# A written-out order of a decoder layer, rewritten with the buffers' spots in it: 45 steps moved by a few places

## The chip, the cores and the metric

The kernel runs on one core of one Trainium2 chip. The core has engines that work side by side, each through its own instructions in order: TensorE (PE in the profile, its weight loads PEld) multiplies matrices, VectorE (DVE) and ScalarE (ACT) do elementwise work, GpSimd (POOL) does some more of it, and SyncE (SP) issues most of the DMA transfers. An instruction waits until what it reads is there and what it overwrites is no longer needed. The metric is the time of one execution on the device in microseconds, as the median of several runs.

## The reference, cut to what matters

The kernel computes one layer of a decoder for 512 positions of width 1024, in float32:

```python
h = rms_norm(x, attn_pre_norm)
mix = hybrid_mixer(h, ...)           # w_in; differential attention (4 heads) and
                                     # sparse attention (8 heads, 3 branches); w_out
x = x + rms_norm(mix, attn_post_norm)
h = rms_norm(x, ffn_pre_norm)
f = (silu(h @ w_gate) * (h @ w_up)) @ w_down      # inner width D_FF = 2816
x = x + rms_norm(f, ffn_post_norm)

def rms_norm(x, g):
    return x * rsqrt(mean(x * x, axis=-1) + 1e-6) * g
```

## The kernel before, in words

All products on TensorE take a value as a high part and a low part, so that float32 accuracy is kept: ScalarE copies the value into a rounded tile (`high_...`, `..._hi`), VectorE subtracts that copy from the value (`low_...`), and TensorE adds up high x high, low x high and high x low.

The first half of the execution, up to about 270 us, is the norm, the projection `w_in` in column groups, the two kinds of attention and the output projection. The second half is the norms and residual between the two, in four row tiles of 128 positions, and the channel mixer. The channel mixer works on 22 tiles of 128 of the inner width (f = 0 to 21):

- `load_ff` loads the gate and up weights of tile f (each 128x1024, 512 KB, line 421), `sum_ff` forms sums and differences of their halves on VectorE (lines 1548 to 1555), `high_ff` (ScalarE, 1568) and `low_ff` (VectorE, 1576) cut them. The products of a gate and an up tile are made from seven `block` products instead of eight (1591). The blocks are numbered 1 to 7, each made of three groups of four matmuls; block 4 is the one with the operand `d` (`dh`, `dl` in the profile), whose third group needs `low_ff.f.d`.
- `snap_1` and `snap_2` copy accumulators out of PSUM (ScalarE, 1621 for the second), `sum_x` (1610) and `sums` (VectorE, 1626) add such a copy to an accumulator, `gate_x` and `gate_c` apply silu, `mult` (1632) multiplies. `sums.f` reads the bank `yz` of tile f, into which block.f.4 afterwards adds its own product: block.f.4 has to wait for `sums.f`.
- For the down projection two tiles of f are taken as a pair p (0 to 8), again by sums and seven products. `pair_sums` adds the activations of the pair (1652) and sends one tile and one sum to DRAM (1654, 1658), to be read back later by `load_b` and `load_s4` (1756). `load_d.f` (421) and `load_22.p` (1676, half a tile) load the down weights; `sums_a.p.0` to `.2` (1682, 1684, 1688) form sums of them. `left_a` and `right_a` cut activations and weights (on VectorE lines 1699 and 1708), `high_d` and `low_d` (1720) the weight tiles as they are, `cut_act` (1792) and `cut_b` further parts. `product_a` and `product_b` are the products (1665). The four tiles f = 18 to 21 also have direct products (`down`, 1814).
- `last_sum`, `last_square`, `last_mean`, `last_gain`, `last_root`, `last_row` are the last norm and residual, by row tile i and column half c.

The norm between (rows i = 0 to 3) has the steps `sa`, `va`, `ra` (`square`, `mean`, `root` of the mixed rows, VectorE line 1454 adding two partial sums of squares of ScalarE), `gu` (`scale_post`, 1477), `re` (residual, with a store), `sb`, `vb`, `rb`, `pr` (`scale_pre`, 1484), `tr` (eight transposes on TensorE, 1514), and `h...`, `l...` (`put_high`, `put_low`, 1507), which cut the transposed rows.

Loaded weight tiles lie in three buffers of the name `wraw`, so a load waits until the last reader of its buffer's former content is done; the high and low parts `whi`, `wlo` have three each as well. Other tiles have a place in tables (`HOMES`, `S_HOMES`), one letter for each use in turn.

No scheduler orders the work. Two long strings of step names, `PLAN` (1387 steps, the attention half) and `PLAN_NORM` with `PLAN_END` (1198 steps, from the norm on) are run from left to right, and each step issues its instructions when it is called. Thus the string gives each engine, and each queue of DMAs, its order. An SP transfer that waits for its buffer holds all transfers behind it in SP's queue; the same is true of VectorE and ScalarE.

Of the kernel before, what the change touches and what calls it, by code (L numbers as in the profile page):

```python
# [61 lines left out]
v0d2 fR10 F11.0 F11.1 pW0 Kh11 D0LD1 KX11 F11.2 F12.0 KX00 Kl11 Kp11 D0S10 D0S11 fR11 D0S12 D0Q12 v0d1 pA5 pH5 D0Q11
pL5 D0X12 KW12 Kh12 Kl12 D0X13 D0Q10 F12.1 F12.2 fL13 fh13 F13.0 fl13 F13.1 F13.2 KW13 Kh13 fR12 D0LD0 Kl13 KX12
Kp12 fL14 D0S00 KX13 Kp13 fR13 fh14 D0S01 KW00 fl14 pA6 D0E13 F14.0 F14.1 Kh00 F14.2 Kl00 fL6 fh6 D0X10 KX01 D0X11
pW5 pH6 D0E12 KW01 Kh01 F6.0 fl6 pL6 D0E11 v0a0 Kl01 D0E10 D0R Kp00 Kp01 KX03 K21 fR14 fL15 fh15 fl15 KW02 Kh02 Kl02
F6.1 pW6 KX02 KO1 F15.0 N0LD F6.2 fR6 KW03 Kh03 Kl03 fL7 F15.1 F15.2 fR15 pA7 N0K1 fh7 Kp02 Kp03 N0S11 D0S02 KO0 KT0
# [20 lines left out]
LW5 v1d3 N3PH N3E10 N3E11 D2Q00 D2X02 D2S10 D2X00 D2X01 N2T00 D2Q11 D2Q10 D2X11 D2X12 D2E02 D2X10 N2H00 N2T02 N2H02
N2L02 N2T01 N2H01 N2L00 D2S12 N4LD N2L01 N1V10 N1V11 N1V12 D2E12 D2Q12 D2X13 N2M10 N2T10 D2E11 N1O1 D2E10 N3M01
N3S12 N2H10 N1O2 N4SC N1OH W6a N4CX N4CA N3PL N3Q12 N2TC N3X13 N2HC N2L10 N2T11 N2H11 D2E13 N3M03 v1p2.0 D2E00 N2L11
N1OL N3S11 D2R N5LD N5SC W1h N3Q11 N5CX D2E01 N3TC D2g N3X12 N2T12 D2MX2 D2MX0 N4K0 D2MX1 N3E13 N3E12 N3R1 N3g1  # L90
v1p2.1 v1a2 v1d2 N3M11 N2H12 N3HC N4S01 N4CE N4K1 N4S1 N3T02 W5h W5l N4Q01 N2L12 N4Q1 N4X11 N4X01 N4E01 N2V00 N4X02
# [2055 lines left out]
```

## Time and profile before

| | |
|---|---|
| median of 3 runs | 623.32 us (621.71 to 624.0) |
| the profiled execution | 622.45 us, span 620.5 us |
| mean granted TensorE clock | 0.994 |
| PE busy | 607.1 us (98%) |
| DVE busy | 546.4 us (88%) |
| ACT busy | 373.9 us (60%) |
| POOL busy | 101.4 us (16%) |
| moved by DMA | 98.41 MB, mean 159 GB/s |

How to read it: the span runs from the first to the last instruction of the profiled execution, and its 1.95 us more are outside of that. "Busy" is the sum of an engine's instructions. A row of the timeline shows the start, the length, the engine, the line of the kernel, the operation, out<-in by the program's names, the shape, how many instructions are taken together (x8), and in brackets the idle time just before and what ended it. SPq is the queue of SP, where a row is the issue of a transfer.

### The profile page before, as it was taken

To read this page: it belongs to the slowest core of one execution; us is meant where nothing else is said; L and a number is where in the kernel's file an instruction comes from. 1 tells how busy PE (TensorE), PEld (TensorE's weight loads), DVE (VectorE), ACT (ScalarE), POOL (GpSimd) and SP (SyncE) were. 2 spreads that over 40 slices of the span, in tenths; PEclk is the share of its full clock that TensorE was granted. 3 is DMA by queue.
4 is the path that set the end of the run, shared out by engine and by line. 5 is a ranking of instruction groups with operands and counts; after the bars stand their busy time and mean duration, and the time that the engine had idled before them with its cause. 6 is when DMAs were issued, how large, how long until landed. Compare 5 with 4: busy or idle time off the path is not lost. (4 is left out here: it accounts for less than half of the span.)

```text
span 620.5 us, 10992 instructions
## 1 busy us (share of the span) xinstructions
PE 607.1 (98%) x4065; PEld 549.9 (89%) x4065; DVE 546.4 (88%) x965; ACT 373.9 (60%) x784; POOL 101.4 (16%) x153
## 2 busy tenths in 40 slices
PE   9999999999999999999999999999999799999995
PEld 5888888899999988889999999999999788878884
DVE  5898898997898884999999998899999699899977
ACT  6445375467999986577584565446464365577522
POOL 0030000307868878100000000000000000000000
PEclk9999999999999999999999999999999989999998
DMA  8566986646233211545143434353531554677413
GB/s 263 187 224 248 299 296 230 216 146 248 101 119 101 88 34 63 182 165 203 59 146 104 156 117 136 119 178 121 175 102 54 174 165 140 201 222 252 135 41 130
DMA packets 38341, 98.41 MB, mean 159 GB/s; under 512 B 4240, under 2 KB 11792, under 8 KB 37392
## 3 DMA queue, kind: packets, MB, share of 16 engines
q1 hardware_dynamic: 38144, 97.59, 47.3%
q8 instruction: 32, 0.52, 0.3%
q14 instruction: 21, 0.17, 0.1%
q10 hardware_dynamic: 144, 0.13, 0.1%
HBM read 82.10 MB, written 15.60 MB: 157 GB/s over the span
## 5 line engine op out<-in xcount | busy, mean ns | idle before, releaser
L1867 POOL TENSOR_TENSOR uf<-c,gain 128x512 f32<-128x512 f32 x1 | 1.3, 1277 | 360.1 <-DVE c L1836 360.1
L1055 ACT ACTIVATE p<-sc,nm 128x512 f32<-128x512 f32 (+3 forms) x96 | 50.2, 530 | 14.4 <-DVE nm L1051 12.9
L1051 DVE TENSOR_REDUCE nm<-sc 128x1 f32<-128x384 f32 (+3 forms) x96 | 43.4, 483 | 8.6 <-PE sc L1047 5.5
L1591 PE MATMUL yz<-rope,wbh 128*128 128x256 f32 x352 | 48.0, 280 | 0.0
L1224 POOL TENSOR_TENSOR p<-p,l 128x256 f32<-128x256 f32 (+3 forms) x64 | 45.3, 732 | 1.0
L1591 PEld LDWEIGHTS yz<-rope,wbh 128*128 128x128 f32 x352 | 44.1, 191 | 0.1
L1085 DVE TENSOR_TENSOR ptl<-tr,pth 128x384 fp32r<-128x384 f32 (+1 forms) x60 | 34.3, 592 | 8.4 <-ACT pth L1082 8.4
L1082 ACT ACTIVATE pth<-tr 128x384 fp32r<-128x384 f32 (+1 forms) x60 | 29.9, 530 | 7.3 <-PE tr L1072 6.8
L1568 ACT ACTIVATE whi<-wraw 128x1024 fp32r<-128x1024 f32 x22 | 23.2, 1057 | 13.3 <-DMA wraw<-in_wg 12.5
L1568 ACT ACTIVATE wbh<-wraw 128x1024 fp32r<-128x1024 f32 x22 | 23.3, 1057 | 12.6 <-DVE wraw L1555 7.7
L1576 DVE TENSOR_TENSOR wel<-e,weh 128x1024 fp32r<-128x1024 f32 x22 | 26.7, 1219 | 3.9 <-ACT weh L1568 2.6
L1568 ACT ACTIVATE weh<-e 128x1024 fp32r<-128x1024 f32 x22 | 23.2, 1056 | 8.0 <-DVE e L1550 6.9
L1072 PE MATMUL tr<-ident,p 128*128 128x128 f32 x200 | 27.8, 274 | 0.0
L1714 ACT ACTIVATE whi<-wraw 128x1024 fp32r<-128x1024 f32 x20 | 21.0, 1057 | 10.9 <-PE acc L1665 5.7
L1591 PE MATMUL yz<-rope,wbl 128*128 128x256 f32 x176 | 27.2, 276 | 0.0
L1576 DVE TENSOR_TENSOR wlo<-wraw,whi 128x1024 fp32r<-128x1024 f32 x22 | 26.8, 1217 | 0.0
L1576 DVE TENSOR_TENSOR wbl<-wraw,wbh 128x1024 fp32r<-128x1024 f32 x22 | 26.7, 1217 | 0.0
L1720 DVE TENSOR_TENSOR wlo<-wraw,whi 128x1024 fp32r<-128x1024 f32 x20 | 24.1, 1218 | 1.1 <-ACT whi L1714 1.1
L1621 ACT ACTIVATE us<-yz 128x512 f32<-128x512 f32 x22 | 13.0, 592 | 18.7 <-PE yz L1591 15.7
L1591 PEld LDWEIGHTS yz<-rope,wbl 128*128 128x128 f32 x176 | 23.4, 188 | 0.0
L1041 PE MATMUL sc<-kst,qst 128*128 128x384 f32 (+3 forms) x64 | 23.0, 367 | 0.3 <-DMA kst<-qk 0.3
L1072 PEld LDWEIGHTS tr<-ident,p 128*128 128x128 f32 x200 | 22.4, 141 | 0.7
(382 smaller groups left out, 1993.9 us busy)
## 6 DMA issues: line engine op xcount, KB each, us to landing
wraw<-in_wg SPq DMA_DIRECT2D x24, 512.0 KB, 3.7
wraw<-in_wu SPq DMA_DIRECT2D x22, 512.0 KB, 3.4
wraw<-in_wd SPq DMA_DIRECT2D x22, 512.0 KB, 3.7
qk<-rope SPq DMA_DIRECT2D x7, 1024.0 KB, 5.9
kst<-qk SPq DMA_DIRECT2D x24, 256.0 KB, 4.2
wraw<-in_wf SPq DMA_DIRECT2D x10, 512.0 KB, 4.2
wraw<-in_wo SPq DMA_DIRECT2D x8, 512.0 KB, 4.4
qst<-qk SPq DMA_DIRECT2D x16, 256.0 KB, 2.7
```

The lines of the kernel that those rows point to most:

```text
L1041: pe.matmul(sv[i], lhs, kk[:, 0, :w], start=(n == 0), stop=False, skip_group_check=True)
L1051: dve.tensor_reduce(nm[i], sv[i], AX.X, OP.max, negate=True)
L1055: act.activation(pp[i], sv[i], AF.Exp, bias=nm[i], accum_out=hs["l"][:, row, i:i + 1])
L1072: pe.transpose(tr[:, n * P:(n + 1) * P], pp[i][:, j * P:(j + 1) * P], ident)
L1082: act.activation(part(u, 0), tv[u], AF.Copy)
L1085: dve.tensor_tensor(part(u, 1), tv[u], f32(part(u, 0)), OP.subtract)
L1224: pool.tensor_tensor(p, p, hs["l"][:, 1 + br, i:i + 1].to_broadcast(list(p.shape)), OP.mult)
L1568: act.activation(t[0], w[src], AF.Copy)
L1576: dve.tensor_tensor(t[1], W[f][PARTS[n][0]], f32(t[0]), OP.subtract)
L1591: pe.matmul(o, W[f][w][wi][:, k * P:(k + 1) * P], hop[h][hi][:, k * HS:(k + 1) * HS], start=(n < 3 and m == 0), stop=(m == 11), skip_group ...
L1714: act.activation(hi, oa[f]["raw"], AF.Copy)
L1720: dve.tensor_tensor(lo, o["raw"], f32(o["w"][0]), OP.subtract)
```

## The change: what it does

The tables of places go. Each step of the two plans names the buffers that it takes itself, as letters behind a colon (`low_d.2:1` takes the spot 1 of its kind), and a new class hands them out. The addresses are the same as before. With the plans rewritten in this way, the order in each engine's own list stays the same for TensorE and GpSimd, and changes a little for three others:

- **SP, 5 of 215 transfers:** `load_s4.1` goes behind `load_22.1` and `load_d.2`. LW1 (a weight of the output projection) goes behind pW3's transfer, `load_ff.3.g` goes two places ahead, in front of the store of re2 and xL3, the store of re3 behind load_ff.2.u, and the row of `last_row.1.1` behind that of last_row.1.0.0.
- **VectorE, 36 of 858 steps.** In the order of the work: Kl13, fR7 and N7CM of the attention's projections and copies by one or two places, N5CX two places down (behind N3X12 and D2MX2); sum_ff.1.1 one down; `gu2` behind l0.11 and sa2, sa2 itself behind l0.11; ra2 and rb2 one down; `sum_x.3` five down, behind sum_ff.4.4; sum_ff.4.3, sums.1 (three), sum_ff.6.4, sum_x.6, sum_ff.8.4, sum_x.5, sum_x.12 (two), pair_sums.3.1 down; sum_ff.18.2 two up; sums.16, mult.13, pair_sums.6.1, low_ff.19.e down; mult.16 four up; `low_d.2` one down, behind `sums.18`; sums_a.4.2 and right_a.7.1.1 one down; `sums_a.8.2` one and `right_a.7.0.1` two down, both behind `right_a.8.1.1`, the latter also behind low_d.16; cut_act.18.1, cut_b.2.2.1 and low_d.13 one down; last_gain.3.0 behind last_mean.3.0, last_sum.0.1 behind last_gain.0.0, `last_gain.1.0` behind last_mean.1.1, last_row.1.1 behind last_row.1.0.0.
- **ScalarE, 4 of 624 steps:** fh10 and Kh13 one down (behind the rotations KX10, KX12), D3LE two up, gate_x.14 one down, behind high_ff.18.e.

The core of the diff (in the plan's lines some neighbours are written in another order that changes no engine's list):

```diff
-wL2 tr00 sb1 h0.11 vb1 rb1 pr11 pr10 h0.12 mx26 mx27 gu2 tr11 kl00 sa2 tr10 mx34 l0.11 h1.11 mx35 mx32 mx33 mx36
...
-pair_sums.6.3 load_s4.1 left_a.0.0.0 load_22.1 left_a.0.0.1 right_a.0.0.0 left_a.2.0.0 pair_sums.7.2 snap_2.21
...
-block.20.6 high_ff.21.b low_ff.21.b block.19.2 high_ff.19.d low_ff.19.d load_d.2 sums_a.1.0 pair_sums.6.4
...
-right_a.1.1.0 right_a.1.1.1 sums_a.1.2 high_d.2 low_ff.21.d low_d.2 high_ff.18.d sums.18 low_ff.18.d block.19.4
...
-right_a.8.1.0 cut_b.2.1.0 low_d.3 sums_a.8.1 sums_a.8.2 high_d.16 right_a.7.0.1 load_b.0 right_a.8.1.1 product_a.7.7
...
-last_square.1.0.1 last_gain.1.0 last_mean.1.1 last_root.1 last_row.1.1 last_row.1.0.0 last_row.1.0.1
...
+kl00:i mx27 tr11:72 l0.11 sa2:4 gu2:8 tr10 mx34 mx35 h1.11 va2 load_ff.3.g:1 mx32 wH0:21 l0.12 mx33 ra2 wH2:10 re2 xL3:d
...
+high_d.0:1 block.21.6 left_a.0.0.0:h9 sums.17:z right_a.0.1.1 block.17.4 load_22.1:1 low_d.0:0 right_a.0.0.0
+left_a.2.0.0 snap_2.21:n pair_sums.7.1:d load_d.2:0 pair_sums.6.3 block.20.6 left_a.0.0.1 high_ff.21.b:gi
+high_ff.19.d:ut gate_c.17 pair_sums.7.2 gate_x.17 load_s4.1:w low_ff.21.b low_ff.19.d block.19.2:5 block.20.5
+block.21.2:3 sums_a.1.0 pair_sums.6.4:x pair_sums.7.4 snap_2.20:4 high_ff.20.d:st mult.17 load_d.4:2 sums_a.1.1
...
+high_ff.18.d:yv sums.18:0 low_d.2:1 low_ff.18.d sums_a.2.0 block.21.3 right_a.2.1.0:1i block.20.3 block.18.4 block.20.7
...
+low_d.3:2 sums_a.8.1 cut_b.2.1.0:4 high_d.16:1 product_a.7.7 load_b.0:t load_kept.3:f right_a.8.1.1 sums_a.8.2:5
+product_a.8.7 low_d.16:0 left_a.8.0.0 right_a.7.0.1 product_a.8.1 cut_b.1.0.0:c left_a.8.0.1 right_a.8.0.0 product_a.8.5
...
+last_square.1.0.0 last_mean.1.0 last_sum.1.0.1 last_square.1.0.1 last_mean.1.1 last_gain.1.0 last_root.1 last_row.1.0.0
+last_row.1.1 last_row.1.0.1
...
+class Spots:
+
+
+    def __init__(self, pool, tags, turn):
+        self.pool, self.tags, self.turn = pool, tags, turn
...
+    def tile(self, shape, dt, tag=None, name=None, bufs=1):
+        if tag in self.tags:
+            return self.pool.tile(shape, dt, tag=f"{tag}.{next(self.turn[0])}", name=name, bufs=1)
+        return self.pool.tile(shape, dt, name=name, bufs=bufs, **({"tag": tag} if tag else {}))
...
+    def run(plan):
+        for step in plan:
+            name, _, spots = step.partition(":")
+            turn[0] = iter(spots)
+            ops[name]()
+            assert not list(turn[0]), step
...
-    for tok in plan:
-        ops[tok]()
+    run(plan)
```

More of the change, by code (lines that the diff above doesn't have):

```diff
@@ L62 @@
[L62 to L66, printed above, removed]
@@ L87 @@
[L87 to L91, printed above, removed]
@@ L177 @@
-block.19.3 high_ff.21.e low_ff.21.e gate_c.14 sum_x.15 gate_x.15 mult.14 sum_x.17 block.21.1 high_ff.21.d
-sum_ff.21.3 gate_c.15 mult.15 block.21.5 snap_1.21 load_22.0 snap_1.20 load_d.0 sums_a.0.0 right_a.0.1.0 sums_a.0.1
-sums_a.0.2 block.19.7 sums.19 block.20.2 block.21.6 sums.17 block.17.4 right_a.0.1.1 high_d.0 low_d.0 pair_sums.7.1
-pair_sums.6.3 load_s4.1 left_a.0.0.0 load_22.1 left_a.0.0.1 right_a.0.0.0 left_a.2.0.0 pair_sums.7.2 snap_2.21
-block.20.6 high_ff.21.b low_ff.21.b block.19.2 high_ff.19.d low_ff.19.d load_d.2 sums_a.1.0 pair_sums.6.4
@@ L182 @@
-pair_sums.7.4 gate_c.17 gate_x.17 mult.17 block.20.5 snap_2.20 high_ff.20.d block.21.2 sums_a.1.1 sum_x.20 load_d.4
-right_a.1.1.0 right_a.1.1.1 sums_a.1.2 high_d.2 low_ff.21.d low_d.2 high_ff.18.d sums.18 low_ff.18.d block.19.4
-block.21.7 load_22.2 load_d.6 sums_a.2.0 right_a.2.1.0 gate_c.19 block.21.3 sums.21 sums_a.2.1 block.20.3 sums_a.2.2
-left_a.6.0.0 right_a.2.1.1 block.18.4 gate_c.18 block.20.7 product_a.0.5 block.21.4 low_ff.20.d sums.20 block.20.4
-left_a.0.1.0 high_d.4 low_d.4 load_22.3 gate_c.21 cut_b.3.2.0 left_a.5.0.0 left_a.0.1.1 product_a.0.7 left_a.2.1.1
@@ L197 @@
-left_a.5.1.1 product_a.5.1 sums_a.6.0 sums_a.6.1 sums_a.6.2 product_a.4.7 product_a.5.7 right_a.6.1.0 load_d.14
-right_a.6.1.1 left_a.6.0.1 cut_b.5.1.0 high_d.12 low_d.12 load_s4.0 cut_b.0.2.0 cut_b.0.2.1 load_22.7 right_a.5.0.1
-sums_a.7.0 left_a.7.0.0 cut_b.4.2.0 sums_a.7.1 load_b.2 right_a.6.0.0 right_a.6.0.1 load_d.16 sums_a.7.2
-product_a.5.6 right_a.7.1.0 right_a.7.1.1 product_a.6.5 left_a.6.1.0 left_a.6.1.1 cut_b.2.2.0 high_d.14 low_d.14
-left_a.7.1.1 gate_x.18 product_a.6.1 mult.18 gate_x.19 load_b.7 left_a.7.0.1 cut_act.18.0 left_a.8.1.1 product_a.6.7
@@ new lines @@
+block.21.2:3 sums_a.1.0 pair_sums.6.4:x pair_sums.7.4 snap_2.20:4 high_ff.20.d:st mult.17 load_d.4:2 sums_a.1.1
+right_a.1.1.0:db sum_x.20:x right_a.1.1.1 block.19.4 sums_a.1.2 block.21.7 load_22.2:1 high_d.2:2 low_ff.21.d
+high_ff.18.d:yv sums.18:0 low_d.2:1 low_ff.18.d sums_a.2.0 block.21.3 right_a.2.1.0:1i block.20.3 block.18.4 block.20.7
+gate_c.19:5 left_a.6.0.0:85 product_a.0.5:27 gate_c.18 sums.21:2 block.21.4 sums_a.2.1 load_d.6:0 sums_a.2.2:g
+left_a.0.1.0 right_a.2.1.1 low_ff.20.d sums.20:v high_d.4:0 block.20.4 low_d.4:2 left_a.0.1.1 left_a.2.1.1 load_22.3:1
```

564 lines of the change are left out of this document (223 added, 341 removed).

## The prediction

> **What bounds the kernel now.** I read the busy shares first, then TensorE's list of waits, then the timelines of TensorE, VectorE and the SP queue around the one large wait.
>
> ```profile
> span 620.5 us, 10992 instructions
> ## 1 busy us (share of the span) xinstructions
> PE 607.1 (98%) x4065; PEld 549.9 (89%) x4065; DVE 546.4 (88%) x965; ACT 373.9 (60%) x784; POOL 101.4 (16%) x153
> ```
>
> TensorE is busy for 607.1 of 620.5 us, and the change leaves its order as it is. So a moved step can only shorten a wait of TensorE, or make one. Its waits by releaser (total, times, longest):
>
> ```profile
> PE yz L1591 <- DVE vs L1626: 3.4, 1, 3.4
> PE warm L543 <- DVE warm L540: 1.2, 1, 1.2
> PE yz L1591 <- DVE wlo L1576: 0.5, 1, 0.5
> ```
>
> Only one is worth much. TensorE's timeline there (start, length, shape, what it waited for):
>
> ```profile
> 491.02 1.07 PE L1591 MATMUL yz<-rope,wbh 128*128 128x256 f32 x8
> 491.92 0.62 PE L1591 MATMUL yz<-rope,wbl 128*128 128x256 f32 x4
> 495.96 0.74 PE L1591 MATMUL yz<-x22h,dh 128*128 128x256 f32 x4 [3.42 <-DVE vs L1626]
> 496.50 1.06 PE L1591 MATMUL yz<-x22l,dh 128*128 128x256 f32 x4
> 497.36 1.05 PE L1591 MATMUL yz<-x22h,dl 128*128 128x256 f32 x4
> 498.21 1.86 PE L1591 MATMUL yz<-rope,wbh 128*128 128x256 f32 x8
> 499.91 0.64 PE L1591 MATMUL yz<-rope,wbl 128*128 128x256 f32 x4
> ```
>
> block.18.4 could have started at 491.92 + 0.62 = 492.54 and starts at 495.96, because `sums.18` (line 1626) must first have read the bank. And then TensorE is slow for 3.4 us. The windows (length, busy time and count of PE, PEld, DVE, ACT, POOL, then the granted clock):
>
> ```profile
> 489.10:492.50 3.40, 3.40 (x31) 3.24 (x29) 2.37 (x6) 2.41 (x4) 0.00 (x0) 1.00 0.59 182
> 492.60:495.90 3.30, 0.00 (x0) 0.00 (x0) 3.30 (x6) 0.34 (x1) 0.00 (x0) 1.00 0.32 119
> 496.50:499.90 3.40, 3.40 (x18) 3.40 (x17) 3.37 (x6) 2.73 (x6) 0.00 (x0) 0.50 0.35 129
> ```
>
> The clock is 0.50 there. Eight of these products took 491.92 − 491.02 = 0.90 us before the wait. The sixteen from 496.50 to 499.91 took 3.41 instead of 2 × 0.90 = 1.80: 1.61 lost, and about 0.1 more in the group at 495.96 (0.54 to the next start instead of 0.45). The place costs 3.42 + 1.7 = 5.1 us in all.
>
> [...]
>
> Why VectorE is late: the SP queue's timeline; then what two loads of a down tile took from issue to landing (last column), the first issued at 482.58, the second a lone one issued between 469.5 and 473; then VectorE.
>
> ```profile
> 481.69 0.33 SPq L1756 DMA_DIRECT2D s4b<-s  x1
> 482.11 0.38 SPq L1676 DMA_DIRECT2D wraw<-in_wd  x1
> 482.58 0.38 SPq L421 DMA_DIRECT2D wraw<-in_wd  x1
> ```
>
> ```profile
> wraw<-in_wd SPq DMA_DIRECT2D x1, 512.0 KB, 5.6
> ```
>
> ```profile
> wraw<-in_wd SPq DMA_DIRECT2D x1, 512.0 KB, 3.4
> ```
>
> ```profile
> 479.96 1.22 DVE L1720 TENSOR_TENSOR wlo<-wraw,whi 128x1024 fp32r<-128x1024 f32 x1
> ```
>
> ```profile
> 488.25 0.69 DVE L1682 TENSOR_TENSOR wraw<-wraw 128x512 f32<-128x512 f32 x1 [3.73 <-DMA wraw<-in_wd]
> ```
>
> ```profile
> 493.99 1.22 DVE L1720 TENSOR_TENSOR wlo<-wraw,whi 128x1024 fp32r<-128x1024 f32 x1
> 495.13 0.68 DVE L1626 TENSOR_TENSOR vs<-yz,us 128x512 f32<-128x512 f32 x1
> 495.73 0.68 DVE L1576 TENSOR_TENSOR dl<-d,dh 128x512 fp32r<-128x512 f32 x1
> ```
>
> `load_s4.1` (line 1756) stands first in the queue and waits for block.17.4's memory until 481.69; `load_22.1` (1676) and `load_d.2` (421) are behind it. load_d.2 goes out at 482.58, though its buffer was free when `low_d.0` ended: 479.96 + 1.22 = 481.18. It lands at 482.58 + 5.6 = 488.2, VectorE idles 3.73 us before sums_a.1.0 (488.25), and all that follows on VectorE is late. Right ahead of sums.18 stands `low_d.2` (493.99), which nothing needs so soon.
>
> **The change, part by part.**
>
> *The queue.* `load_s4.1` moves behind load_22.1 and load_d.2. load_d.2 then goes out at 481.21, 1.37 earlier, and load_22.1 before it. How long it flies no row shows. The bounds are 5.6 (as now, between two others) and 3.4 (the lone one); I take 4.0, near the lone one, because the 256 KB store and load that crowd it now start after it and only load_22.1, ahead of it, shares its way. It lands at 485.21, 0.04 after it sums_a.1.0 starts: 488.25 − 485.25 = 3.0 earlier; I count S = 2.95 (bounds 1.35 and 3.55). What cover is left: VectorE has other work until 484.5, so a landing earlier than that would gain nothing.
>
> *low_d.2 behind sums.18.* sums.18 moves up by 495.13 − 493.99 = 1.14. With both, it ends at 495.13 + 0.68 − 2.95 − 1.14 = 491.72, before 492.54: no wait. block.18.4's third group needs `low_ff.18.d`, which ends now at 495.73 + 0.68 = 496.41 and then at 493.46; at full speed the third group starts 492.54 + 2 × 0.45 = 493.44. Just in time. So 5.1 us are free at this place; with a flight of 5.6, low_ff.18.d ends at 495.06 and a wait of some 1.6 is left, too short, going by what is seen here after 3.42, to be sure of a slow clock.
>
> *What is late next.* TensorE, 5.1 earlier from here, meets the next VectorE limit. From 496 to 550 VectorE stays close behind. Where it waits for TensorE now, it gains back more than S:
>
> ```profile
> 500.58 0.69 DVE L1626 TENSOR_TENSOR vs<-yz,us 128x512 f32<-128x512 f32 x1 [0.38 <-PE yz L1591]
> ```
>
> ```profile
> 514.36 0.69 DVE L1699 TENSOR_TENSOR sl<-s,sh 128x512 fp32r<-128x512 f32 x1 [0.39 <-PE acc L1665]
> ```
>
> Both waits shrink, since TensorE gains more than VectorE: 2.95 + 0.38 + 0.39 = 3.72 by 515. The point where TensorE then stops is product_a.8.7, whose third operand comes from `right_a.8.1.1`:
>
> ```profile
> 544.94 0.69 DVE L1688 TENSOR_TENSOR t<-wraw 128x512 f32<-128x512 f32 x1
> 545.55 0.68 DVE L1708 TENSOR_TENSOR tl<-t,th 128x512 fp32r<-128x512 f32 x1
> 546.15 0.68 DVE L1708 TENSOR_TENSOR tl<-wraw,th 128x512 fp32r<-128x512 f32 x1
> ```
>
> ```profile
> 546.13 0.39 PE L1665 MATMUL acc<-th,sh 128*128 128x512 f32 x1
> 546.36 0.40 PE L1665 MATMUL acc<-th,sl 128*128 128x512 f32 x1
> 546.89 0.50 PE L1665 MATMUL acc<-tl,sh 128*128 128x512 f32 x1
> ```
>
> At a start every 0.23 us TensorE would take it at 546.59 and gets it 0.30 late, at 546.89. In the change `sums_a.8.2` (544.94) and `right_a.7.0.1` (545.55) go behind right_a.8.1.1: 546.15 − 544.94 = 1.21 earlier on VectorE, of which 0.30 goes to that lateness. TensorE can so come 1.21 − 0.30 = 0.9 more than VectorE's gain: 3.72 + 0.9 = 4.6. That is under 5.1, so the place at 546 caps it. I take 4.6; with S at its bounds 1.35 and 3.55 it is 1.35 + 0.77 + 0.9 = 3.0 and, past the cap, 5.1.
>
> *gu2 behind sa2.* VectorE:
>
> ```profile
> 276.54 0.16 DVE L1454 TENSOR_TENSOR cols<-cols 128x1 f32<-128x1 f32 x1 [0.82 <-ACT pre L1452]
> ```
>
> ```profile
> 292.94 0.74 DVE L1484 SCALAR_TENSOR_TENSOR pre<-x,cols,gain 128x512 f32<-128x512 f32 x1
> ```
>
> ```profile
> 293.21 1.18 PE L1514 MATMUL trh<-ident,pre 128*128 128x128 f32 x8
> ```
>
> ```profile
> 315.64 0.62 PE L1591 MATMUL yz<-x11l,whi 128*128 128x256 f32 x4
> 316.36 0.74 PE L1591 MATMUL yz<-x11h,wlo 128*128 128x256 f32 x4
> ```
>
> The two products of `gu2` (scale_post, 1477) now fill time before sa2's wait for ScalarE (0.82); behind it they leave that much more idle time, less the 0.69 subtraction that steps into it. I put VectorE 0.7 late from there (bounds 0 and 0.82). scale_pre ends at 293.68, 0.05 before the second four transposes, so TensorE may stop 0.65 at 293. Two later waits of TensorE take that up: the 0.5 of the list above (low_ff.16.a, its line 1576), which is shorter when TensorE comes later, and at 316, where the third group starts 316.36 − 315.64 − 0.45 = 0.27 late for low_ff.4.a; there `sum_x.3`, moved five places down, lets low_ff.4.a come sooner. Together 0.77. I cost it at 0, and at 0.65 if that cover is gone.
>
> *The rest.* N5CX goes behind D2MX2, which waits for GpSimd's D2g; no wait of TensorE's list is for line 1208: 0 to 0.2. The other VectorE, ScalarE and SP steps (Kl13, fR7, N7CM, the sum_ff, sum_x and sums neighbours, mult.13 and .16, left_a and cut_b, fh10, Kh13, D3LE, gate_x.14, LW1, re3's store, load_ff.3.g) swap with one to four neighbours, each late or early by that neighbour's length (0.2 to 1.22); no wait of TensorE over 0.5 stands by any of them. In the tail, last_mean.1.1 goes ahead of last_gain.1.0, which frees the root and the last rows by a tenth, and last_row.1.1 goes behind last_row.1.0.0: −0.1 to +0.2, taken as 0.
>
> **The sum** is −4.6 + 0 + 0 = −4.6. The profiled execution of before is 622.45 (span 620.5 and 1.95 around it); it becomes 617.85. It stands 0.87 under the median of 623.32, so the median becomes 623.32 − 4.6 = **618.7**. Its own range, with the bounds of the flight: 623.32 − 5.1 = 618.2 to 623.32 − 3.0 = 620.3.
>
> **The rivals.**
>
> *A: the wait goes, the slow clock isn't part of the gain.* The timed runs may not have it, or it may fall elsewhere. For it: the runs before differ by 2.3 us (621.71 to 624.0), more than the 1.7 that it costs. Against it: the wait of 3.42 must be in each of them, by the same order. Only the wait is then gained: 623.32 − 3.4 = 619.9.
>
> *B: load_d.2 lands no sooner.* If the DMA engines, and not the queue, set the landing at 488.2 (5.6 us for a load that takes 3.4 alone says that they are shared), sums_a.1.0 stays at 488.25. Only low_d.2's move is left, and the third group still waits for low_ff.18.d at 496.41: the wait is split, not removed. TensorE gains the first two groups done meanwhile, 2 × 0.45 = 0.9 at most: 622.4, or, with half of that lost to the slow clock, 622.9. Against it: the DMA share in the windows is 0.32 to 0.59, not near full.
>
> *C, the other side: gu2's lateness reaches TensorE and stays.* VectorE, 0.7 late behind gu2, stops TensorE for 0.65 at 293. If the two waits don't take it up (VectorE may be as late there, and then they only move along) and the place at 492 returns nothing, the time is 623.32 + 0.65 = 624.0. It decides from the point where VectorE is over 0.05 late at 293.68 and what 492 returns is under 0.65. For it: 0.05 is little room. Against it: load_d.2 is free to go 1.37 sooner, twice that sum.
>
> *That the change doesn't do what it says* (another address, and so another wait) would show as a new wait anywhere; I give it a part of C's chance.
>
> **How the numbers follow.** Forecast 0.66, A 0.12, B 0.14, C with the last 0.08. The predicted time is the forecast's, 618.7. The range leaves out most of B and C (under 0.2): 617.0 (the 5.1 in full, and 1.2 for how the three runs before lie about their median) to 622.0 (the forecast's and A's upper ends and 1.7 of that spread and of flights between 4.0 and 5.6). About 0.5%, 3.1 us, is what a measurement here can tell from no change: 620.2 and below is faster. The forecast lies there in 0.93 of its cases, A in 0.6: 0.66 × 0.93 + 0.12 × 0.6 = 0.69. Slower by 3.1 takes C and a new stop with a slow clock after it: 0.05. The remaining 0.26 is the same.
>
> **What would show it.** In the changed profile, load_d.2's row should be issued at about 481.2 and ahead of s4b's; VectorE's idle time before line 1682 at 485.3 should be 0.8, not 3.73; the list of TensorE's waits should have no vs row of 3.4, and no window near 496 a clock of 0.50. TensorE should run 5.1 ahead until 540 and keep 4.6 after 546, with a wait of about half a us for `tl`, line 1708. A landing at 488, a large wait of L1591 for `dl`, or TensorE late at 293 and still late at 450, would each prove a step wrong.

## The result, and the profile after

The changed kernel took 617.03 us (median of 4 runs, 616.62 to 618.48), the kernel before 623.28 beside it: a ratio of 0.9907, 95% interval 0.9883 to 0.9932. Timed again later beside other kernels it took 616.95 against 623.48: 0.9897 (0.9873 to 0.9920). It is faster by 6.3 to 6.5 us where 4.6 were forecast; 617.03 lies 0.03 inside the low end of the range, the second median just outside it. Of the timed runs below one, of g4, was slow throughout (667.49 us at a mean clock of 0.948); it stands in that kernel's median but not in its ratio, and its trace is not used.

The profiled execution took 618.48, the slowest of the four. The page's head and TensorE's waits:

```profile
span 616.6 us, 11000 instructions
## 1 busy us (share of the span) xinstructions
PE 605.2 (98%) x4065; PEld 548.2 (89%) x4065; DVE 545.2 (88%) x965; ACT 373.8 (61%) x784; POOL 101.0 (16%) x153
```

```profile
PE yz L1475 <- DVE vs L1510: 1.3, 1, 1.3
PE warm L425 <- DVE warm L422: 1.2, 1, 1.2
PE fm L590 <- ACT whi L577: 0.9, 1, 0.9
PE yz L1475 <- DVE dl L1460: 0.5, 1, 0.5
```

The lines of the second half have moved up by 116: 1475 is the former 1591, 1510 the former 1626, 1460 the former 1576 (and 310 is the helper at 421). The wait of 3.4 us for `vs` has become one of 1.3 and one of 0.5 for `dl`, and the 0.5 for `wlo` is down to 0.2. The 0.9 at line 590 (F13.0, at 72 us) belongs to this execution: the same kernel profiled again (f1) doesn't have it. TensorE's timeline at the place:

```profile
491.59 0.62 PE L1475 MATMUL yz<-rope,wbl 128*128 128x256 f32 x4
493.47 0.71 PE L1475 MATMUL yz<-x22h,dh 128*128 128x256 f32 x4 [1.27 <-DVE vs L1510]
494.02 0.63 PE L1475 MATMUL yz<-x22l,dh 128*128 128x256 f32 x4
495.11 0.72 PE L1475 MATMUL yz<-x22h,dl 128*128 128x256 f32 x4 [0.46 <-DVE dl L1460]
495.67 1.07 PE L1475 MATMUL yz<-rope,wbh 128*128 128x256 f32 x8
```

and the windows (length, PE, PEld, DVE, ACT, POOL, clock, DMA share, GB/s):

```profile
491.15:494.56 3.41, 2.14 (x18) 1.86 (x16) 3.38 (x6) 0.31 (x1) 0.00 (x0) 1.00 0.37 123
494.56:497.97 3.41, 2.95 (x22) 2.68 (x22) 3.38 (x6) 2.19 (x6) 0.00 (x0) 1.00 0.47 154
497.97:501.38 3.41, 3.41 (x28) 3.33 (x27) 3.41 (x6) 2.32 (x6) 0.00 (x0) 1.00 0.55 186
```

The clock stays at 1.00; the eight products at 495.67 take 0.91 to the next start, against the 0.90 at full speed in before. What led there, the SP queue, the flight of load_d.2 and VectorE:

```profile
480.04 0.33 SPq L1560 DMA_DIRECT2D wraw<-in_wd  x1
481.18 0.33 SPq L310 DMA_DIRECT2D wraw<-in_wd  x1
481.56 0.42 SPq L1640 DMA_DIRECT2D s4b<-s  x1
```

```profile
wraw<-in_wd SPq DMA_DIRECT2D x1, 512.0 KB, 5.1
```

```profile
486.38 0.69 DVE L1566 TENSOR_TENSOR wraw<-wraw 128x512 f32<-128x512 f32 x1 [1.89 <-DMA wraw<-in_wd]
...
490.37 0.42 DVE L1494 TENSOR_TENSOR act<-x,snap 128x256 f32<-128x256 f32 x1 [1.42 <-DMA s<-s]
...
492.63 0.69 DVE L1510 TENSOR_TENSOR vs<-yz,us 128x512 f32<-128x512 f32 x1
493.24 1.21 DVE L1604 TENSOR_TENSOR wlo<-wraw,whi 128x1024 fp32r<-128x1024 f32 x1
494.37 0.68 DVE L1460 TENSOR_TENSOR dl<-d,dh 128x512 fp32r<-128x512 f32 x1
```

load_22.1 and load_d.2 go out at 480.04 and 481.18, s4b behind them, as forecast. But the flight is 5.1 us, VectorE still idles 1.89 and begins 1.87 sooner, not 2.95. Then `sum_x.20` (490.37) idles 1.42 for the store of s4. In f1, the same kernel again, load_d.2 flew 4.2:

```profile
wraw<-in_wd SPq DMA_DIRECT2D x1, 512.0 KB, 4.2
```

Where TensorE gains, place by place, can be read by the start of the same step in each trace. The table gives that start less its start in the profile of before, in us (minus: earlier). e1, e2 and e4 are the experiments below, f1 is the changed kernel profiled a second time, f3, f4 and g1 are variants of it.

| step | before, at | e1 | e2 | changed | f1 | e4 | f3 | f4 | g1 |
|---|---|---|---|---|---|---|---|---|---|
| F10.0 | 52.52 | −0.28 | −0.43 | −0.37 | −0.69 | −0.38 | −0.54 | −0.54 | −0.44 |
| D0T2 | 122.98 | −0.28 | +0.59 | +1.09 | −0.73 | +0.06 | +0.05 | −0.58 | −0.08 |
| D0MS | 147.08 | −0.31 | +0.59 | +0.68 | −1.13 | −0.37 | −0.35 | −1.01 | −0.52 |
| tr20 | 286.87 | −0.25 | +0.53 | +0.71 | −1.18 | −0.20 | −0.47 | −1.14 | −0.36 |
| tr30 | 293.73 | −0.25 | +0.55 | +0.62 | −1.27 | −0.29 | +0.40 | −1.23 | −0.45 |
| block.15.5 | 416.26 | +0.37 | +0.64 | +0.67 | −1.04 | −0.13 | +1.01 | −1.34 | −0.07 |
| block.16.2 | 425.22 | +0.67 | +0.38 | +0.17 | −1.84 | −0.93 | +0.21 | −2.14 | −0.16 |
| block.20.6 | 481.50 | +0.77 | +0.66 | −0.34 | −2.35 | −1.44 | −0.30 | −2.65 | −0.67 |
| product_a.0.5 | 500.38 | −3.13 | −0.63 | −3.35 | −6.20 | −1.06 | −4.17 | −7.94 | −4.02 |
| product_a.6.1 | 537.78 | −3.14 | −0.66 | −3.06 | −5.92 | −0.71 | −3.93 | −6.82 | −3.80 |
| down_piece.21.1 | 612.66 | −3.39 | −1.06 | −3.47 | −6.33 | −1.13 | −4.34 | −7.23 | −4.22 |

Up to 123 us the columns differ by up to 1.8 us with no pattern by kernel; that is how one execution differs from the next (the changed kernel itself is at +1.09 and, in f1, at −0.73), and it is why the profile of the changed kernel (+1.09 there) shows less than the times. Differences between two rows of one column are what counts. From 481 to 500 the changed kernel gains 3.0 and 3.85. But it also gains some 0.4 between 123 and 147, 0.5 to 0.8 at 425 and about 0.5 from there to 481. The first is in no profile of the old order, and none of these gains more than 0.3 at 425; of the last e3, which has the old order there, shows 0.4 too (+1.55 to +1.16), so it may not be the change's.

### The profile page after: what moved, and what is told of

The parts are those of the page before. It is cut to its first block, busy times and chain, and to the rows that moved or that the text cites. A ratio compares the mean times of both kernels' runs of the same rounds, so it can differ in the third digit from the quotient of the medians.

```text
span 616.6 us, 11000 instructions
## 1 busy us (share of the span) xinstructions
PE 605.2 (98%) x4065; PEld 548.2 (89%) x4065; DVE 545.2 (88%) x965; ACT 373.8 (61%) x784; POOL 101.0 (16%) x153
## 4 chain that ended last, share of the span: by engine, by line
PE 31%; DVE 15%; DMA 3%; issue 2%; ACT 1%; DVEq 0%; ACTq 0%
PE yz L1475 15%; PE acc L1549 12%; PE x L1475 2%; DMA wraw<-in_wd 2%; DVE wbl L1460 1%; DVE wlo L1460 1%; PE acc L1698 1%; DVE wel L1460 1%; DVE c L1720 1%; DVE wlo L1604 1%; DVE uf L1755 1%; DVE e L1432 1%; DMA wraw<-in_wg 1%; DVE dl L1460 1%; DVE e L1434 1%
```

## The experiments

### The load, and low_d.2: each alone, both, and all the rest

e1, e2 and e3 are the kernel before with one or both of the two moves near 481 and 494; e4 is the changed kernel without these two.

e1, against the kernel before:

```diff
-pair_sums.6.3 load_s4.1 left_a.0.0.0 load_22.1 left_a.0.0.1 right_a.0.0.0 left_a.2.0.0 pair_sums.7.2 snap_2.21
-block.20.6 high_ff.21.b low_ff.21.b block.19.2 high_ff.19.d low_ff.19.d load_d.2 sums_a.1.0 pair_sums.6.4
+pair_sums.6.3 left_a.0.0.0 load_22.1 left_a.0.0.1 right_a.0.0.0 left_a.2.0.0 pair_sums.7.2 snap_2.21
+block.20.6 high_ff.21.b low_ff.21.b block.19.2 high_ff.19.d low_ff.19.d load_d.2 load_s4.1 sums_a.1.0 pair_sums.6.4
```

e2 (e3 has both edits):

```diff
-right_a.1.1.0 right_a.1.1.1 sums_a.1.2 high_d.2 low_ff.21.d low_d.2 high_ff.18.d sums.18 low_ff.18.d block.19.4
+right_a.1.1.0 right_a.1.1.1 sums_a.1.2 high_d.2 low_ff.21.d high_ff.18.d sums.18 low_d.2 low_ff.18.d block.19.4
```

e4, against the changed kernel:

```diff
-high_d.0:1 block.21.6 left_a.0.0.0:h9 sums.17:z right_a.0.1.1 block.17.4 load_22.1:1 low_d.0:0 right_a.0.0.0
+high_d.0:1 block.21.6 left_a.0.0.0:h9 sums.17:z right_a.0.1.1 block.17.4 load_s4.1:w load_22.1:1 low_d.0:0 right_a.0.0.0
...
-high_ff.19.d:ut gate_c.17 pair_sums.7.2 gate_x.17 load_s4.1:w low_ff.21.b low_ff.19.d block.19.2:5 block.20.5
+high_ff.19.d:ut gate_c.17 pair_sums.7.2 gate_x.17 low_ff.21.b low_ff.19.d block.19.2:5 block.20.5
...
-high_ff.18.d:yv sums.18:0 low_d.2:1 low_ff.18.d sums_a.2.0 block.21.3 right_a.2.1.0:1i block.20.3 block.18.4 block.20.7
+high_ff.18.d:yv low_d.2:1 sums.18:0 low_ff.18.d sums_a.2.0 block.21.3 right_a.2.1.0:1i block.20.3 block.18.4 block.20.7
```

> The kernel before with load_s4.1 alone behind load_d.2 in SP's queue; all else as before. Theory 1 (the place at 492 carries the gain): load_d.2 is issued at 481.2 instead of 482.6 and lands about 1.9 us sooner, as the changed kernel's trace has it (sums_a.1.0 at 486.4 instead of 488.25). sums.18 then ends near 493.9, TensorE's wait falls from 3.42 to about 1.5 and the half clock goes. At 546 right_a.8.1.1 is late again, since sums_a.8.2 and right_a.7.0.1 still stand ahead of it: gain 1.9 + 0.77 - 0.30 = 2.3, median about 621.0 (620.4 to 621.6). Rival (the many small steps elsewhere carry it): the gain is under 1 us, 622.3 or more.

> The kernel before with low_d.2 alone behind sums.18 on VectorE. Theory 1: the wait before block.18.4 falls by 1.14 to about 2.3, but its third group then waits for low_ff.18.d, which ends at 496.4 as before, some 0.7 us; no single wait is 3.4 long any more, so the half clock goes. TensorE gains 2 us at the place, but VectorE hardly any, and the stop for right_a.8.1.1 at 546 takes all but 0.5 back: 622.8 (622.3 to 623.3). If the half clock remains, the same within 0.3.

> The kernel before with both moves and nothing else of the change. Theory 1: as the changed kernel at 492 (two waits of about 1.3 and 0.5 in place of 3.42 and the slow clock, some 3.1 us gained there), with a stop at 546 of about 0.8 for right_a.8.1.1: median 620.7 (620.0 to 621.3). The remaining 3.5 us or so of the 6.25 measured must then be in the other steps (rival). If these two moves were all, 617 to 618.

> The changed kernel with these two moves put back (load_s4.1 ahead of load_22.1, low_d.2 ahead of sums.18). Theory 1 alone: the wait of 3.4 us at block.18.4 and the half clock behind it return, and the time is that of before, 622.5 to 623.3. Rival (the other 43 steps carry part): the wait returns, but the time stays below before by what they are worth, about 619.5 to 621.

Beside 622.59 for the kernel before (26 runs):

| kernel | median us | ratio to before, 95% interval |
|---|---|---|
| e1, load_s4.1 alone | 619.37 | 0.9956 (0.9934 to 0.9978) |
| e2, low_d.2 alone | 622.57 | 0.9991 (0.9974 to 1.0007) |
| e3, both | 619.70 | 0.9938 (0.9917 to 0.9959) |
| e4, the other 43 steps | 620.76 | 0.9963 (0.9948 to 0.9977) |

The load's move alone is worth 3.2 us, more than I had left for it (2.3). low_d.2's shows nothing in the times, alone (0.0, though its interval reaches to 1.6 and its trace gains 1.3 between 481 and 500) or on top of the load's (619.70 against 619.37). The other 43 steps, which the prediction summed to 0, are worth 1.8. TensorE at block.18.4 in e1, e2 and e4:

```profile
494.45 0.70 PE L1591 MATMUL yz<-x22h,dh 128*128 128x256 f32 x4 [1.14 <-DVE vs L1626]
```

```profile
495.29 1.10 PE L1591 MATMUL yz<-x22h,dh 128*128 128x256 f32 x4 [2.09 <-DVE vs L1626]
```

```profile
494.07 1.19 PE L1475 MATMUL yz<-x22h,dh 128*128 128x256 f32 x4 [2.97 <-DVE vs L1510]
```

In e1 one wait of 1.14 is left, and the third group doesn't wait: low_ff.18.d stands behind low_d.2 either way, and it is what the third group needs. When sums.18 goes ahead of low_d.2, as in e3 and the changed kernel, the wait is split into two: 0.5 and 0.5 in e3, in total hardly less than e1's 1.14; 1.27 and 0.46 in the execution above, 0.4 and 0.5 in f1. e4 shows that the wait comes back without the two moves, and that the gain at 425 (−0.13 to −0.93 in the table) stays: it belongs to the rest.

The windows of e2 and e4 show the clock. e2:

```profile
491.98:495.39 3.41, 1.32 (x12) 1.15 (x12) 3.16 (x6) 0.93 (x2) 0.00 (x0) 1.00 0.48 165
495.39:498.80 3.41, 3.41 (x16) 3.41 (x17) 3.38 (x6) 1.22 (x3) 0.00 (x0) 0.50 0.52 170
```

and e4:

```profile
489.87:493.28 3.41, 1.23 (x11) 1.03 (x10) 3.32 (x6) 0.70 (x2) 0.00 (x0) 1.00 0.42 155
493.28:496.69 3.41, 2.62 (x12) 2.65 (x13) 3.21 (x7) 1.22 (x3) 0.00 (x0) 0.50 0.53 183
496.69:500.10 3.41, 3.41 (x16) 3.30 (x15) 2.35 (x4) 2.05 (x4) 0.00 (x0) 0.50 0.28 80
500.20:503.60 3.40, 3.40 (x27) 3.21 (x26) 3.37 (x7) 0.90 (x3) 0.00 (x0) 1.00 0.48 145
```

In e2 a stretch at half clock came after a wait of 2.09 us. That it would go once no wait is 3.4 long was an assumption in e2's expectation, and the run shows otherwise. In e4 the stretch lasts 6.8 us (493.28 to 500.10). The prediction called a wait of 1.6 "too short" for it only by what 3.42 had shown; what the runs say of it stands in the last section.

### The changed kernel again, without the three moves near 546, without gu2's, and with less wait

f2, against the changed kernel:

```diff
-low_d.3:2 sums_a.8.1 cut_b.2.1.0:4 high_d.16:1 product_a.7.7 load_b.0:t load_kept.3:f right_a.8.1.1 sums_a.8.2:5
-product_a.8.7 low_d.16:0 left_a.8.0.0 right_a.7.0.1 product_a.8.1 cut_b.1.0.0:c left_a.8.0.1 right_a.8.0.0 product_a.8.5
-load_d.1:0 cut_act.18.1:o product_a.7.6 cut_b.1.2.0:1 cut_b.6.2.0:0 high_d.1:2 right_a.8.0.1 sums_b.0 cut_b.6.2.1
+low_d.3:2 sums_a.8.1 cut_b.2.1.0:4 high_d.16:1 product_a.7.7 load_b.0:t load_kept.3:f sums_a.8.2:5 right_a.7.0.1 right_a.8.1.1
+product_a.8.7 low_d.16:0 left_a.8.0.0 product_a.8.1 cut_b.1.0.0:c cut_act.18.1:o left_a.8.0.1 right_a.8.0.0 product_a.8.5
+load_d.1:0 product_a.7.6 cut_b.1.2.0:1 cut_b.6.2.0:0 high_d.1:2 right_a.8.0.1 sums_b.0 cut_b.6.2.1
```

f3:

```diff
-kl00:i mx27 tr11:72 l0.11 sa2:4 gu2:8 tr10 mx34 mx35 h1.11 va2 load_ff.3.g:1 mx32 wH0:21 l0.12 mx33 ra2 wH2:10 re2 xL3:d
-mx36 h1.12 mx37 wl0 sb2 l1.12 wl2 vb2 l1.11 rb2 pr20 B2.2:6 pr21 B1.2:0 kl01 sa3:5 kl11:3 high_ff.3.a:10 tr20:35 k212:3
+kl00:i mx27 tr11:72 gu2:8 sa2:4 l0.11 tr10 mx34 mx35 h1.11 va2 load_ff.3.g:1 mx32 wH0:21 ra2 l0.12 mx33 wH2:10 re2 xL3:d
+mx36 h1.12 mx37 wl0 sb2 l1.12 wl2 vb2 rb2 l1.11 pr20 B2.2:6 pr21 B1.2:0 kl01 sa3:5 kl11:3 high_ff.3.a:10 tr20:35 k212:3
```

f4:

```diff
-right_a.1.1.0:db sum_x.20:x right_a.1.1.1 block.19.4 sums_a.1.2 block.21.7 load_22.2:1 high_d.2:2 low_ff.21.d
-high_ff.18.d:yv sums.18:0 low_d.2:1 low_ff.18.d sums_a.2.0 block.21.3 right_a.2.1.0:1i block.20.3 block.18.4 block.20.7
+right_a.1.1.0:db right_a.1.1.1 block.19.4 sums_a.1.2 block.21.7 load_22.2:1 high_d.2:2 low_ff.21.d sum_x.20:x
+high_ff.18.d:yv sums.18:0 low_ff.18.d low_d.2:1 sums_a.2.0 block.21.3 right_a.2.1.0:1i block.20.3 block.18.4 block.20.7
```

> The changed kernel itself, timed beside the next three. What is known by now: the load's move alone gave 3.2 us, the other 43 steps 1.8, and low_d.2's alone nothing. If the two sums add up, the median is 5.0 below the kernel before, 617.6 where that takes 622.6. Mean granted clock in its runs 0.997 to 0.998: no slow stretch in the middle.

> The changed kernel with sums_a.8.2, right_a.7.0.1 and cut_act.18.1 back at their places of before (ahead of right_a.8.1.1 and left_a.8.0.1). The prediction's step: right_a.8.1.1 comes 1.21 later, TensorE stops for it at product_a.8.7 near 543, and 0.6 to 0.9 us of the gain is lost. Rival (what the trace with the load's move alone shows, where VectorE was 3.4 earlier at 542 and TensorE didn't wait): VectorE has regained its lateness by then, no wait of TensorE for tl over 0.3, and the time stays within 0.4.

> The changed kernel with gu2 ahead of sa2 and l0.11, ra2 ahead of l0.12 and rb2 ahead of l1.11, as before. The prediction's step: VectorE is some 0.7 earlier at 293 without the move, and TensorE isn't stopped there by it in either kernel; the time stays within 0.3. Rival C (the move costs 0.65 that is taken up later): TensorE's lead at 293 against the changed kernel grows by 0.6, and is gone by 425. If the lead stays, the kernel is 0.6 faster.

> The changed kernel with sum_x.20 behind low_ff.21.d on VectorE, where it waits 1.42 for the store of s4 with work behind it that is ready, and low_d.2 also behind low_ff.18.d. If the two waits left at block.18.4 (1.27 for sums.18, 0.46 for low_ff.18.d) are what is left to gain there, sums.18 ends 1.2 to 1.4 earlier, TensorE waits under 0.3 us in all, and the time is 1.2 to 1.7 below the changed kernel. If VectorE's own chain to 514 is the bound, TensorE stops again before 520 and under 0.6 is kept.

Beside 623.48 for the kernel before (11 runs):

| kernel | median us | ratio to before, 95% interval |
|---|---|---|
| f1, the changed kernel | 616.95 | 0.9897 (0.9873 to 0.9920) |
| f2, moves near 546 back | 616.77 | 0.9897 (0.9874 to 0.9919) |
| f3, gu2's moves back | 618.05 | 0.9922 (0.9898 to 0.9947) |
| f4, less wait | 615.54 | 0.9873 (0.9851 to 0.9896) |

f1: the load's 3.2 and the rest's 1.8 add up to 5.0; the changed kernel gains 6.5, with an interval from 5.0 to 7.9. The sum lies at its edge, but its terms have intervals too (1.4 to 4.1 and 1.4 to 3.2), so a difference is not shown.

f2: nothing is lost in the time, and no wait for `tl` is in TensorE's list. In the trace TensorE gains 0.2 at 546 where f1 gains 0.4, so the three moves are worth some 0.2 there. In e3, which lacks them too, the limit does show, by as much as in the kernel before (0.30):

```profile
PE acc L1665 <- DVE tl L1708: 0.3, 1, 0.3
```

It binds by some tenths at most, not by the 0.6 to 0.9 that the prediction's step would take.

f3: its median is 1.1 us above f1's, the other way round from the forecast, with intervals that overlap. What the forecast had missed stands in the trace of before. ScalarE's square of row tile 2, in before, in f1 and in f3:

```profile
275.06 0.60 ACT L1452 ACTIVATE pre<-mix 128x512 f32<-128x512 f32 x1 [1.22 <-DVE u L1477]
```

```profile
273.16 0.60 ACT L1336 ACTIVATE pre<-mix 128x512 f32<-128x512 f32 x1 [0.50 <-PE mix L1222]
```

```profile
275.15 0.60 ACT L1336 ACTIVATE pre<-mix 128x512 f32<-128x512 f32 x1 [1.77 <-DVE u L1361]
```

The squares read the same `mix` tiles as gu2's products, and with gu2 written first ScalarE waits for it; sa2 on VectorE then waits for ScalarE. So the idle 0.82 that I let stay behind l0.11 was made by gu2 itself. With gu2 behind sa2, the squares wait for TensorE alone and sa2 doesn't wait at all. In f3 TensorE also stops at 293 for scale_pre:

```profile
293.24 0.63 PE L1398 MATMUL trh<-ident,pre 128*128 128x128 f32 x4 [0.16 <-DVE pre L1368]
294.14 0.66 PE L1398 MATMUL trh<-ident,pre 128*128 128x128 f32 x4 [0.27 <-DVE pre L1368]
```

Its column goes from −0.47 at tr20 to +0.40 at tr30, 0.87 lost; in f1 it goes from −1.18 to −1.27. But this is f3's own: before, e1 and e2, which have the old order unchanged, lose nothing there. f3's ra2 waits 0.46 for ScalarE, which it doesn't in before:

```profile
277.87 0.22 DVE L1351 SCALAR_TENSOR_TENSOR cols<-cols 128x1 f32<-128x1 f32 x1 [0.46 <-ACT x11h L1388]
```

The move itself is read better against before. The scale_pre that frees the second four transposes, in f1 and in f3:

```profile
291.47 0.74 DVE L1368 SCALAR_TENSOR_TENSOR pre<-x,cols,gain 128x512 f32<-128x512 f32 x1
```

```profile
293.34 0.74 DVE L1368 SCALAR_TENSOR_TENSOR pre<-x,cols,gain 128x512 f32<-128x512 f32 x1
```

Counted from tr20 of its own trace it ends 6.81 us later in before (293.68), 6.52 in f1 and 7.68 in f3. So the move makes VectorE 0.29 earlier at 293, not 0.7 late, takes sa2's wait away, shortens ScalarE's from 1.22 to 0.50, and gives TensorE 0.1 there. f3 is no measure of it.

f4 is 7.9 below the kernel before and, by the medians, 1.4 below f1; the intervals overlap, but g4 below, which has the same edit, repeats it. block.18.4 starts without a wait, and of TensorE's list little is left:

```profile
489.72 0.62 PE L1475 MATMUL yz<-x22h,dh 128*128 128x256 f32 x4
```

```profile
PE warm L425 <- DVE warm L422: 1.2, 1, 1.2
PE yz L1475 <- DVE vs L1510: 0.3, 1, 0.3
```

From product_a.0.5 to product_a.6.1 it gives back 1.1 (−7.94 to −6.82 in the table). Half of that is lost where the wait of 0.3 for `vs` stands, so VectorE bounds there in part; 0.3 more f1 gives back as well.

### sum_x.12, LW1 and s4's load

g1, against the changed kernel:

```diff
-gate_c.8 low_ff.14.b low_ff.14.a block.13.5 block.12.3 high_ff.13.b:hc gate_x.5 snap_1.13:5 sum_x.12:i mult.6
+gate_c.8 sum_x.12:i low_ff.14.b low_ff.14.a block.13.5 block.12.3 high_ff.13.b:hc gate_x.5 snap_1.13:5 mult.6
```

g2:

```diff
-D1Q00 D1X11:3 v1p0.0:3 N0M11 v1p0.1 D1E11:0 pW3 N0M03 D1E12:2 v1a0:n LW1:0 N0M01 D1X01:1 N0PL N0T02:7 N0T00:2 D1X00:7
+D1Q00 D1X11:3 v1p0.0:3 N0M11 v1p0.1 D1E11:0 LW1:0 pW3 N0M03 D1E12:2 v1a0:n N0M01 D1X01:1 N0PL N0T02:7 N0T00:2 D1X00:7
```

g3 (g4 has this edit and f4's):

```diff
-high_ff.19.d:ut gate_c.17 pair_sums.7.2 gate_x.17 load_s4.1:w low_ff.21.b low_ff.19.d block.19.2:5 block.20.5
-block.21.2:3 sums_a.1.0 pair_sums.6.4:x pair_sums.7.4 snap_2.20:4 high_ff.20.d:st mult.17 load_d.4:2 sums_a.1.1
+high_ff.19.d:ut gate_c.17 pair_sums.7.2 gate_x.17 low_ff.21.b low_ff.19.d block.19.2:5 block.20.5
+block.21.2:3 sums_a.1.0 pair_sums.6.4:x pair_sums.7.4 snap_2.20:4 high_ff.20.d:st mult.17 load_d.4:2 load_s4.1:w sums_a.1.1
```

> The changed kernel with sum_x.12 back ahead of low_ff.14.b and low_ff.14.a, where in the kernel before it idled 0.58 us for the store of s. Theory (that wait, with ready work behind it, made TensorE's wait of 0.5 for low_ff.16.a at 425): the wait of VectorE returns, TensorE waits 0.5 to 0.8 at 425 again, and the time is 0.5 to 0.8 above the changed kernel. Rival (the gain at 425 is gu2's, carried along on VectorE): TensorE doesn't wait there and the time stays.

> The changed kernel with LW1 back ahead of the store of pW3 in SP's queue. In all six profiles with the changed order TensorE gains 0.4 us between 123 and 147, in the four with the old order 0.0. Theory: that is the transfer pW3 no longer standing behind LW1, and the 0.4 goes. Rival: it is another step of the attention half, and the 0.4 stays in the profile. In the time it is too little to be told.

> The changed kernel with load_s4.1 behind load_d.4 too, so that its 256 KB don't run beside load_d.2. The prediction took 4.0 us for load_d.2's flight, the changed kernel's profiles show 4.2 to 5.1. If the load behind it crowds it, the flight falls by up to 1 us, sums_a.1.0 starts as much sooner, and the time is 0.3 to 0.9 lower. If it is the stores of the activations (two of 256 KB) or nothing that orders can change, the flight stays within 4.2 to 5.1 and the time within 0.3.

> The kernel with sum_x.20 behind low_ff.21.d and low_d.2 behind low_ff.18.d, which took 615.54, with load_s4.1 behind load_d.4 as well. Only 0.3 us of TensorE's wait is left there, so no more than 0.3 can be gained: 615.2 to 615.6.

Beside 623.13 for the kernel before: g1 616.78 (0.9892, 0.9863 to 0.9921), g2 616.77 (0.9890, 0.9863 to 0.9918), g3 616.86 (0.9897, 0.9870 to 0.9924), g4 615.20 (0.9869, 0.9840 to 0.9899).

g1: the step in the trace is there. sum_x.12 waits for the store of s in before and again in g1, and TensorE waits for line 1460 (list of g1):

```profile
402.28 0.43 DVE L1610 TENSOR_TENSOR act<-x,snap 128x256 f32<-128x256 f32 x1 [0.58 <-DMA s<-s]
```

```profile
402.47 0.42 DVE L1494 TENSOR_TENSOR act<-x,snap 128x256 f32<-128x256 f32 x1 [0.63 <-DMA s<-s]
```

```profile
PE yz L1475 <- DVE wlo L1460: 0.8, 2, 0.4
```

From block.15.5 to block.16.2 g1 gains 0.09 where f1 gains 0.80. But its median is not above the changed kernel's, so in the time these 0.7 us are not shown; the medians of the kernel before differ by as much from series to series (622.59 to 623.48).

g2: the 0.4 between 123 and 147 stays (0.07 to −0.36 in its trace). It isn't LW1, and which step it is stays open. g3: the flight of load_d.2 is 5.0 with s4's load out of the way, within the 4.1 to 5.1 of the profiles that have it behind, and the time is the same. So nothing shows that this load crowds it, though one flight in a spread of 1 us can't rule out a small share. g4 has the lowest median of all, but is no different from f4 by what these runs can tell.

## Why the prediction was right, and where its steps were wrong

The direction, the place and the main cause were right: the wait at block.18.4 came from load_d.2 standing in SP's queue behind s4's load, and moving that load gave half of what was gained. The time came out 1.7 us lower than forecast, since errors on both sides partly cancelled: the place gave less than 4.6 (3.0 and 3.9 between 481 and 500 in the two profiles), the rest gave 1.8 and more where 0 was put. That the median still fell into the range, by 0.03, is luck. Of the signs that were named, the row issued at 481.2, the vanished wait of 3.4 and the full clock came true; the idle time of 0.8 before sums_a.1.0 (1.89) and the wait for `tl` did not. By its steps:

- **The queue: right, its flight taken too short.** Issued at 481.18 as forecast (481.21), though this trace was 0.34 ahead by then. The flight was put at 4.0, near the lone load's, because a store and a load that crowd it would start after it. That was a misreading in part: the two stores of 256 KB went out behind it in the kernel before as well (at 483.01), so only s4's load changed sides. In the profiles of the changed order the flight was 4.1 to 5.1, and 5.1 in the one shown, whose S was 1.87, near the low bound of 1.35. The two stores and s4's load go out within 1.4 us behind it and fly along (5.7 and 5.4 us). Nothing shows that s4's load is to blame (g3); that the stores are is only argued, and why the same kernel shows 4.2 and 5.1 stays open.
- **low_d.2: wrong.** "sums.18 moves up by 1.14" came true, and was worth nothing on top of the load's move. The forecast saw that the third group needs low_ff.18.d, but called it just in time with a flight of 4.0. In the changed kernel that group stops for 0.46, and for 0.49 in f1, whose flight was 4.2; in e1, where sums.18 still stands behind low_d.2, it doesn't. What the first wait loses the second takes. So the flight isn't all of it: the prediction carried S undiminished to sums.18 and left out sum_x.20 on the way, whose wait for the store of s4 is in the trace of before and grew to 1.42 in the changed kernel and 1.50 in f1:

```profile
491.85 0.43 DVE L1610 TENSOR_TENSOR act<-x,snap 128x256 f32<-128x256 f32 x1 [1.03 <-DMA s<-s]
```

  The step that helps is low_ff.18.d ahead of low_d.2 with sum_x.20 out of the way (f4); the two were not tried apart.
- **What is late next, the cap at 546: wrong.** It counted 0.77 as regained on VectorE, two waits. The trace of before has another that I left out, and the idle time of 1.68 before sums_a.8.0 (542.41) shrank to 1.26 in e1 as well:

```profile
508.46 1.23 DVE L1720 TENSOR_TENSOR wlo<-wraw,whi 128x1024 fp32r<-128x1024 f32 x1 [0.38 <-ACT whi L1714]
```

  In e1 VectorE is 1.64 earlier at sums_a.1.0 and 3.40 at sums_a.8.0, 1.76 regained. So TensorE keeps its gain with or without the three moves, to 0.2 us (f2) or the 0.3 of e3's wait.
- **gu2: wrong in sign.** "They leave that much more idle time" took sa2's wait as given; it was gu2's own doing, and VectorE is 0.29 earlier at 293 instead of 0.7 late. Rival C rested on the same step: its cost does not exist. The 0 that was put for the step is right to 0.1 us, by another way.
- **"The rest" at 0: wrong.** e4 puts it at 1.8. By the traces of the changed order, 0.5 to 0.8 are at 425 with sum_x.12, listed among "neighbours" though its row showed a wait of 0.58 for a store with ready work behind it. About 0.4 more are at the end. The prediction gave the swap of last_mean.1.1 and last_gain.1.0 a tenth; but ScalarE's root waits 0.40 for the mean in before (first row), and in the changed kernel no more:

```profile
615.00 0.29 ACT L444 ACTIVATE rr<-ss 128x1 f32<-128x1 f32 x1 [0.40 <-DVE ss L1857]
```

```profile
610.36 0.40 ACT L1735 ACTIVATE uj<-c 128x256 bf16<-128x256 f32 x1
610.67 0.19 ACT L1735 ACTIVATION_READ_ACCUMULATOR uj<-c 128x1 f32 x1
610.89 0.30 ACT L333 ACTIVATE rr<-ss 128x1 f32<-128x1 f32 x1
```

  Its span ends 0.43 sooner after TensorE's last step than before's does (616.6 against 620.5, with TensorE 3.47 earlier). The same 0.4 is in f1, f4 and e4, and in e1, e2 and e3 there is none. That the swap makes it is argued from these rows; no run tried it alone. The 0.4 between 123 and 147 is in all profiles of the changed order and unexplained.
- **The slow clock: right for this change, and rival A is out.** It was counted once, 1.7 us. That these 1.7 go with the wait was an assumption: no run of before shows it, as the wait of 3.42 and the slow stretch stand there together. In the changed kernel, with waits of 1.27 and 0.46, the clock is 1.00 from 491.15 to 501.38; in e2, with a wait of 2.09, the slow stretch is still there. The mean clock of each timed run gives an estimate of how often it is there: the profiles without a slow stretch have a mean of 0.996 to 0.998, that of before with 3.4 us of it 0.994, that of e4 with 6.8 us 0.992. Of the 48 runs of the kernel before beside e1 to g4, 6 have a mean of 0.996 (median 621.2 us), 25 of 0.993 to 0.995 (622.5) and 17 of 0.991 or 0.992 (623.9). By this estimate half of the runs have about 3.4 us of it and a third about 6.8, while all ten runs of the changed kernel have 0.996 to 0.998.
- **Rival B** (no sooner landing) is out: 486.38 against 488.25, and e1's time.

Against the forecast's −4.6, the load gave −3.2, low_d.2 0 and the rest −1.8; all together gave −6.3 to −6.5. The 1.3 to 1.5 between the sum and the whole lie within the intervals. The traces leave less of a gap: e1 gains 3.9 between 481 and 500 (+0.77 to −3.13), and the rest 0.4 between 123 and 147, 0.5 to 0.8 at 425, 0.5 from there to 481 (if that is the change's) and 0.4 at the end, 5.7 to 6.0 in all. In e4 the place itself costs 0.4 more than in before, its slow stretch being 6.8 us long against 3.4, so that its 1.8 puts the rest somewhat low.

## What to carry to other kernels

In an order written by hand, look for a waiting instruction with ready work behind it: here four such places that were cleared (a load behind a blocked load, sum_x.12 behind a store, sum_x.20 behind a store together with low_d.2, the root behind a gain's product) gave 0.4 to 3.9 us in the trace, and each had its own row with a wait in the profile. Not each one pays: sa2's wait of 0.82 went, and TensorE gained 0.1. Before a wait is carried over into the new order, ask who makes it: the neighbour that is moved past it may be its cause, as gu2 was through ScalarE. When a wait for a producer is removed, follow the next operand of the same consumer before counting the gain.

## What the runs showed of the hardware

At block.18.4 a stretch at half clock came with waits of TensorE of 3.42 us (before), 2.97 (e4) and 2.09 (e2), none with 1.27 and 0.46 (the changed kernel) nor with 1.14 (e1). By the windows it was 3.4 us long in before (1.00 up to 496.47, 0.50 to 499.88, 1.00 from 499.90), 6.8 in e4, where it began at 493.28 while TensorE still waited, and e2's window of 3.41 is at 0.50. The runs of one kernel are not alike in this: in 2 of e2's 12 the mean clock is 0.998, as in the profiles without a slow stretch, and in the other ten 0.993 to 0.995. What decides whether the stretch comes, and how long it is, was not shown.

Also unexpected was that ScalarE's square of `mix` waited for VectorE's product of it where the product was written first, though both only read it: 1.22 us in before and 1.77 in f3. In f1, where the square is written first, it waited for TensorE alone (0.50). Whether the chip could do without this wait was not tried.
